# A fifth pair of channels in a feed-forward stage, and weight remainders written by accumulating transfers

## The chip, the cores and the metric

The kernel runs on one core of one Trainium2 chip. A core has TensorE (PE: matmuls and transposes; PEld is its weight load), VectorE (DVE), ScalarE (ACT), GpSimd (POOL) and SyncE (SP), which here only issues transfers. The engines run at the same time, each through its own instructions in order. The metric is the device time of one execution in microseconds, as the median of several runs; lower is better.

## The reference

A decoder trunk of two layers in float32, for 512 tokens of width 1024. The first layer is a Mamba-2 mixer, the second is latent attention; each is followed by a gated feed-forward block, and a layer norm stands behind each of the four.

```python
for i in range(DEPTH):
    if i < N_A_LAYERS:
        mix = ssd_mixer(h, ...)
    else:
        mix = mla_attention(h, q_down[j], q_norm_g[j], q_up[j], attn_out[j], k_nope, k_rope, v, cos, sin)
    h = layer_norm(DN_ALPHA * h + mix, ln_mix_g[i], ln_mix_b[i])
    ff = conv_ffn(h, ffn_up[i], ffn_conv_w[i], ffn_conv_b[i], ffn_down[i])
    h = layer_norm(DN_ALPHA * h + ff, ln_ffn_g[i], ln_ffn_b[i])
    if i == N_A_LAYERS - 1:
        shared_kv = mla_shared_kv(h, kv_down, kv_norm_g, kv_up_k, kv_up_v, cos, sin)

def conv_ffn(h, up, conv_w, conv_b, down):
    u = causal_depthwise_conv(h @ up, conv_w, conv_b)
    g, val = jnp.split(u, 2, axis=-1)
    return (jax.nn.silu(g) * val) @ down
```

The feed-forward block has 2816 hidden channels, 22 groups of 128. The attention has 8 heads, with a query rank of 384, a key/value rank of 256 and a rotary part of 64.

## The kernel before

**Two-part numbers.** TensorE works on a rounded 32-bit format, so each operand is split into a rounded part (`h`, tile `wh` for weights) and a remainder (`l`, tile `wl`). A product is three matmuls: high by high, high by low, low by high (`mm_a` for up projections, `mm_b`, lines 165 to 167, for those with tokens on the rows).

**The weight stream.** `WStream` holds one list of weight items in the order of their use. SyncE loads an item into a staging tile `wst`; `_split` makes `wh` with a ScalarE cast (line 96) and `wl` with a VectorE subtraction (line 97). `wh` and `wl` have six slots each, and an item's slot is free when the product of the item six places earlier is done. `ahead` and `get` say how far ahead of the product the split stands in program order. Items of the kinds "r", "a", "+", "-" are sums and differences of weight blocks, made in a tile `rs` by transfers: the kind "a" is an accumulating transfer that POOL issues (line 52).

**The stages.** The mixer ends at about 412 us. The first feed-forward stage runs to about 770, the attention to about 953, the second feed-forward stage to the end.

**A feed-forward stage** (`ffn`) takes its channel groups in two rounds and then the rest. In a round, the up projection computes channels (two banks of 24 matmuls for each), with convolution, activation and split on ScalarE and VectorE. Neighbouring channels form a pair, and `down_pairs` multiplies the pairs by their down weights with seven products of half-token blocks for two output halves, where the plain way has eight (a Strassen-like scheme: `pair_operands` makes the sums of activations, the weight stream those of weights). The table `RP0` (first stage) or `RP1` (second stage) lists the pairs: ((2, 2, 1), (2, 1, 1)) is five pairs in the first round and four in the second, and numbers in brackets are the pairs that share one weight item. Channels beyond the pairs go through plain pieces (`piece`), one for each token tile of 128 and output half, with the residual add (line 185) and the layer norm behind them: a mean (189), a sum of squares on ScalarE (194), a small POOL part, two steps on VectorE for each half (210 and 215). `transpose_h` turns a normed token tile into `ht` with eight transposes (274), a ScalarE cast (277) and a VectorE subtraction (278). Two tiles are transposed within the stage, two are put off (`k.pend`) into the attention.

**The attention** (`mla`) first projects down (`down`, 16 steps of three matmuls for a token tile, weights `dw`), transposes the compressed rows, and makes V and the rotary queries. Then it goes head by head: `qk` for the next head (weights `hw`, 640 wide, or the staged split of an output weight, 1024 wide, later on), `qk_rope` for every second head, `pv` of the head before (its output is copied to `oT`, ScalarE line 1307, VectorE line 1308), `ptrans` (transposes of the probabilities E to PT, lines 1288 to 1291), `scores` of the next head. Two `ws.ahead` calls in each head place the splits. Last come the output pieces (`out_piece`): the first two items of the output weights `aow` for all token tiles, then, after the last head's `pv`, the other six.

**What sets the order.** Each engine's instructions are put in order by a scheduler at build time; only SyncE's keep the order of the program. `issue_after` ties a split to a point of the other work.

Of the kernel before, what the change touches and what calls it, by code (L numbers as in the profile page):

```python
# [18 lines left out]
P = 128  # L19
# [10 lines left out]

class WStream:


# [42 lines left out]
    def _split(self, nst=None):  # L76
# [19 lines left out]
        nc.scalar.copy(h[:, :f], s[:, :f])  # L96
        nc.vector.tensor_tensor(l[:, :f], s[:, :f], h[:, :f], op=ALU.subtract)  # L97
        self.w[i] = (h, l)
# [188 lines left out]

RP0 = ((2, 2, 1), (2, 1, 1))
RP1 = ((2, 2, 1), (2, 1, 1))


def rounds(rp):
    r0 = 2 * sum(rp[0])
    return r0, r0 + 2 * sum(rp[1])


def ffn_items(up, down, rp):

    it = []
    R0, R1 = rounds(rp)
    dv = down.rearrange("(k p) n -> p k n", p=P)
    for r, ks in enumerate((range(R0), range(R0, HT))):
        for c in ks:
            it.append((up[c], 1024))
            it.append((up[c + HT], 1024))

        for odd, hf, kinds in ((0, 0, "r"), (0, 1, "a"), (1, 1, "+="), (0, 0, "-"), (1, 0, None), (1, 0, "a")):
            j = ks[0]  # L310
            for p, n in enumerate(rp[r]):
                b = dv[:, j:j + 2 * n, hf * 512:(hf + 1) * 512].rearrange("p (k e) n -> p k e n", e=2)[:, :, odd, :]
                it += [(b, n * 512, kind, p) for kind in kinds or (None,)]
                j += 2 * n
    for hf in range(2):
        for j in range(R1, HT, 2):
            it.append((dv[:, j:j + 2, hf * 512:(hf + 1) * 512], 1024))
    return it
# [41 lines left out]

def down_pairs(k, ws, n, prs, parts, first, between):

# [3 lines left out]
    nc = k.nc  # L366
    X, Y, Z = ([k.bank() for _ in range(2)] for _ in range(3))
    ni = len(parts)
# [23 lines left out]
    def ahead(n, ins):  # L392

        with k.tc.issue_after(ins.ins):
            ws.ahead(n)
# [3 lines left out]
    n += ni  # L399
    ahead(n, add(X, 0, 0, 1))  # L400
    for p in range(ni):
        product(Y, "s1", p, n + p, True, True)
    n += ni
    ahead(n, add(Y, 1, 1, 1))
    between()
    for p in range(ni):
        product(X, "s2", p, n + 2 * p, False, True)
        product(Y, "s4", p, n + 2 * p + 1, False, True)
    n += 2 * ni
    add(X, 0, 1, -1)  # L410
    ahead(n, add(Y, 0, 1, 1))
# [8 lines left out]
def ffn(k, ws, base, cwp, gb, rp, la=2, out=None, mid=None):  # L420

    nc, tc = k.nc, k.tc
    R0, R1 = rounds(rp)
    with ExitStack() as c:
        pool = lambda n, b: c.enter_context(tc.tile_pool(name=n, bufs=b))
        pools = {"gt": pool("gt", 18), "fw": pool("fw", 7), "rs": pool("rs", 1), "cw": pool("cw", 1)}
        k.junk = (pools["fw"], "acc")
# [17 lines left out]
        for r in range(2):  # L445
# [5 lines left out]
            def finish(ci, bg, bv):  # L451
# [8 lines left out]
                j = len(prs)  # L460
                a11, a2, s12, s34 = half[j // 2][:, j % 2], new_gt(), new_gt(), new_gt()
                pair_operands(k, pools, even.pop(), av, a11, a2, s12, s34)
# [4 lines left out]
            if k.pend:  # L467
# [19 lines left out]
                c0 += 2  # L487
            for ci in range(c0, HT if r else R0):
                bg, bv = k.bank(), k.bank()
                ws.ahead(n + 1)  # L490
                for b, i in ((bg, n), (bv, n + 1)):
                    w = [x.rearrange("p (k m) -> p k m", k=KT) for x in ws.get(i)]
                    k.mm_a(b, w, k.ht, slice(0, 512))
                    ws.retire(i)
                n += 2
                ws.ahead(n)
                finish(ci, bg, bv)
            if mid and not r:
                mid()
            n = down_pairs(k, ws, n, prs, rp[r], not r, norm_params if r else lambda: None)  # L500
        if out is None:
# [23 lines left out]
        for i in range(NT):  # L525
# [20 lines left out]
            k.add_mix(i, 1, b, 1.0, True)  # L546
            if out is None and i >= 2:
                k.transpose_h(i - 2)
            xn[i] = row("xn")
# [11 lines left out]
    if out is None:  # L561
        k.pend = [lambda: k.transpose_h(NT - 2), lambda: k.transpose_h(NT - 1)]
    return n
# [9 lines left out]
LAG = [20, 18, 7.6, 5, 7.6, 13]  # L573
DRAM = bass.MemoryType.DRAM


# [488 lines left out]
def mla_items(dw, vw, rw, hw, ow):  # L1065

    it = [(dw[j], 1024) for j in range(4)] + [(dw[j][:, :768], 768) for j in (4, 5)]
    rv = rw.rearrange("(k p) n -> p k n", p=P)
    it += [(rv[:, 0:2, :], 1024), (rv[:, 2:3, :], 512)]
    vv = vw.rearrange("(k p) n -> p k n", p=P)  # L1070
    it += [(vv[:, :, hf * 512:(hf + 1) * 512], 1024) for hf in range(2)]
    it += [(hw[h], 640) for h in range(AH)]
    it += [(ow[j * P:(j + 1) * P, :], 1024) for j in range(AH)]
    return it
# [47 lines left out]
def mla(k, ws, base, ngp, gb):  # L1122
    nc, tc = k.nc, k.tc
    with ExitStack() as cx:
# [18 lines left out]

        def down(i):
            bq, bk = k.bank(), k.bank()
# [9 lines left out]
            seen = set()  # L1155
            for c, (j, o, kk, off, w) in enumerate(plan):
                wh, wl = ws.get(n[0] + j)
                last = o.shape[1] == QR and kk == 7 or o.shape[1] != QR and kk == 7
# [59 lines left out]
        for i in range(NT):  # L1218
            down(i)
            if k.pend:  # L1220
                k.pend.pop(0)()
            if i:
                down_t(i - 1)
# [239 lines left out]
```

## Time and profile before

| what | value |
|---|---|
| median of 3 runs | 1312.31 us (1311.85 to 1312.35) |
| profiled execution | 1311.7 us |
| its span in the trace | 1310.0 us |
| granted TensorE clock | 0.998 |
| PE busy | 1299.5 us, 99% of the span |
| DVE busy | 1020.6 us, 78% |
| ACT busy | 636.0 us, 49% |
| POOL busy | 93.1 us, 7% |

A row of the groups, or of the timeline, names a line, an engine, an operation, the tiles written and read, and shapes; a number in brackets at its end is the idle time ahead of it with what ended it. PE's spans are pipelined, so that the pace of matmuls is the distance of their starts. In the chain of waits each row is a start, a length and what the execution's end depended on then.

### The profile page before, as it was taken

The page shows a single profiled execution, that of the slowest core. Times are in us where ns is not written, and L with a number is a line of the kernel's source. Part 1 is how long each engine was busy: PE and PEld are TensorE (multiplying, and loading weights), DVE is VectorE, ACT ScalarE, POOL GpSimd, SP SyncE. Part 2 cuts the span into 40 slices and gives each one's busy share as a digit, 9 for nine tenths or more (in the row PEclk, how much of TensorE's full clock was granted, in tenths as well). Part 3 has the DMA queues.
Part 4 walks back from the last instruction along what each step waited for, and adds up shares of the span by engine and source line. Part 5 has one row for each costly group of instructions (what it writes and reads, how often), then busy time and mean ns, then how long its engine had stood idle before and what let it go on. Part 6 is the DMA issues. An engine that isn't in the chain of part 4 may idle for free.

```text
span 1310.0 us, 17422 instructions
## 1 busy us (share of the span) xinstructions
PE 1299.5 (99%) x6666; PEld 1098.9 (84%) x6666; DVE 1020.6 (78%) x1581; ACT 636.0 (49%) x1029; POOL 93.1 (7%) x96
## 2 busy tenths in 40 slices
PE   9999999999999999999999999999999999999997
PEld 8888888888888988888888899888898888888886
DVE  7888888797798868866766876898587686667587
ACT  6765555455453544444443434665254444444341
POOL 0111011011011001100000012000100010000000
PEclk9999999999999999999999999999999999999999
DMA  8423322313410433352311822121144227323251
GB/s 297 179 113 129 113 88 90 132 58 133 161 65 10 171 129 81 80 207 98 123 58 31 254 81 62 71 107 49 35 149 135 79 35 213 130 97 105 41 161 65
DMA packets 49779, 144.59 MB, mean 110 GB/s; under 512 B 5312, under 2 KB 6336, under 8 KB 48416
## 3 DMA queue, kind: packets, MB, share of 16 engines
q1 hardware_dynamic: 44480, 133.57, 28.8%
q0 software_dynamic: 5072, 9.77, 4.4%
q8 instruction: 52, 0.85, 0.3%
q14 instruction: 31, 0.25, 0.1%
q10 hardware_dynamic: 144, 0.15, 0.0%
HBM read 141.30 MB, written 2.16 MB: 110 GB/s over the span
## 4 chain that ended last, share of the span: by engine, by line
PE 95%; DVE 4%; ACT 1%; issue 0%; DVEq 0%; ACTq 0%
PE ps L159 57%; PE ps L165 10%; PE ps L167 10%; PE ps L166 10%; PE ps L803 1%; PE ps L915 1%; PE ps L811 1%; PE ps L274 1%; PE ps L792 1%; PE ps L742 1%; PE ps L1265 1%; DVE wl L97 1%; DVE PT L1291 1%; PE ps L770 1%; DVE E L1279 0%; DVE smx L1275 0%
## 5 line engine op out<-in xcount | busy, mean ns | idle before, releaser
L159 PE MATMUL ps<-ht,wh 128*128 128x512 f32 (+1 forms) x2256 | 517.0, 379 | 0.0
L159 PEld LDWEIGHTS ps<-ht,wh 128*128 128x128 f32 x2256 | 408.1, 188 | 79.7 <-issue 1.4
L97 DVE TENSOR_TENSOR wl<-wst,wh 128x1024 fp32r<-128x1024 f32 (+3 forms) x222 | 256.3, 1169 | 44.2 <-ACT wh L96 43.3
L96 ACT CAST wh<-wst 128x1024 fp32r<-128x1024 f32 (+3 forms) x222 | 218.8, 995 | 114.3 <-PE ps L167 62.3
L159 PE MATMUL ps<-ht,wl 128*128 128x512 f32 (+1 forms) x1128 | 266.6, 378 | 0.0
L159 PEld LDWEIGHTS ps<-ht,wl 128*128 128x128 f32 x1128 | 205.2, 188 | 39.6
L328 DVE SCALAR_TENSOR_TENSOR acc<-ps,cw,acc 128x511 f32<-128x511 f32 x88 | 65.7, 747 | 80.0 <-ACT acc L327 80.0
L165 PE MATMUL ps<-wh,gt 128*128 128x512 f32 (+1 forms) x320 | 123.7, 387 | 0.0
L167 PE MATMUL ps<-wh,gt 128*128 128x512 f32 (+1 forms) x320 | 123.6, 386 | 0.0
L166 PE MATMUL ps<-wl,gt 128*128 128x512 f32 (+1 forms) x320 | 123.6, 386 | 0.0
L340 ACT CAST gt<-acc 128x512 fp32r<-128x512 f32 (+1 forms) x80 | 44.0, 571 | 102.0 <-DVE acc L333 99.3
L657 DVE SCALAR_TENSOR_TENSOR cv<-ps,cw,cv 128x511 f32<-128x511 f32 (+2 forms) x96 | 71.3, 746 | 26.8 <-ACT cv L655 25.9
L327 ACT ACTIVATE acc<-ps,cw 128x512 f32<-128x512 f32 x88 | 68.3, 776 | 29.5 <-PE ps L159 29.4
L167 PEld LDWEIGHTS ps<-wh,gt 128*128 128x128 f32 x320 | 60.1, 188 | 12.3
L332 ACT ACTIVATE acc<-acc 128x512 f32<-128x512 f32 x44 | 27.8, 632 | 87.6 <-DVE acc L329 87.5
L165 PEld LDWEIGHTS ps<-wh,gt 128*128 128x128 f32 x320 | 60.1, 188 | 12.1
L166 PEld LDWEIGHTS ps<-wl,gt 128*128 128x128 f32 x320 | 60.1, 188 | 12.1
L329 DVE SCALAR_TENSOR_TENSOR acc<-ps,cw,acc 128x510 f32<-128x510 f32 x88 | 65.8, 748 | 2.5
L52 POOL DMA_DIRECT2D rs<-in_down_dram x24 | 25.4, 1058 | 572.7 <-DVE wl L97 572.7
L96 ACT CAST wh<-rs 128x1024 fp32r<-128x1024 f32 (+1 forms) x48 | 39.9, 834 | 46.4 <-DVE rs L88 27.1
L341 DVE TENSOR_TENSOR gt<-acc,gt 128x512 fp32r<-128x512 f32 (+1 forms) x80 | 48.8, 627 | 13.5 <-ACT gt L340 13.5
L387 DVE SCALAR_TENSOR_TENSOR h<-h,ps 128x512 f32<-128x512 f32 x56 | 37.6, 686 | 26.0 <-PE ps L167 26.0
(242 smaller groups left out, 1744.7 us busy)
## 6 DMA issues: line engine op xcount, KB each, us to landing
wst<-in_up_dram SPq DMA_DIRECT2D x88, 512.0 KB, 3.5
wst<-in_xbc_dram SPq DMA_DIRECT2D x32, 512.0 KB, 6.0
wst<-in_down_dram SPq DMA_DIRECT2D x26, 512.0 KB, 5.5
W<-cumd SPq DMA_DIRECT2D x8, 1024.0 KB, 4.6
wst<-in_sow_dram SPq DMA_DIRECT2D x16, 512.0 KB, 3.6
wst<-in_zw_dram SPq DMA_DIRECT2D x14, 512.0 KB, 6.1
rs<-in_down_dram POOLq DMA_DIRECT2D x12, 512.0 KB, 6.9
wst<-in_down_dram SPq DMA_DIRECT2D x18, 256.0 KB, 2.6
```

Source lines behind the costliest of these rows:

```text
L96: nc.scalar.copy(h[:, :f], s[:, :f])
L97: nc.vector.tensor_tensor(l[:, :f], s[:, :f], h[:, :f], op=ALU.subtract)
L159: nc.tensor.matmul(out, w[:, k, :], xts[k][:, x, ts], start=first and p == 0 and k == 0, stop=last and p == 2 and k == nk - 1, skip_group_ ...
L165: nc.tensor.matmul(out, xt[:, 0, tsl], wh, start=start, stop=False, skip_group_check=True)
L166: nc.tensor.matmul(out, xt[:, 0, tsl], wl, start=False, stop=False, skip_group_check=True)
L167: nc.tensor.matmul(out, xt[:, 1, tsl], wh, start=False, stop=stop, skip_group_check=True)
L327: nc.scalar.activation(a, b, AF.Identity, bias=cw[:, ch, 3:4], scale=cw[:, ch, 2:3])
L328: nc.vector.scalar_tensor_tensor(a[:, 1:], b[:, :SEQ - 1], cw[:, ch, 1:2], a[:, 1:], op0=ALU.mult, op1=ALU.add)
L329: nc.vector.scalar_tensor_tensor(a[:, 2:], b[:, :SEQ - 2], cw[:, ch, 0:1], a[:, 2:], op0=ALU.mult, op1=ALU.add)
L340: k.nc.scalar.copy(dst[:, 0, :], src)
L341: k.nc.vector.tensor_tensor(dst[:, 1, :], src, dst[:, 0, :], op=ALU.subtract)
L657: nc.vector.scalar_tensor_tensor(t[:, d:], b[:, :SEQ - d], cw[:, ch, 3 - d:4 - d], t[:, d:], op0=ALU.mult, op1=ALU.add)
```

## The change

`RP0` now has five pairs in both rounds, so that two plain channels are left (20 and 21). The activations' pool holds 18 tiles, too few for everything at once: the two plain channels are computed within `down_pairs`, behind its first product (`late`), two of the banks are taken later, and the load of the norm's parameters (`between`) moves behind two more products. The stage transposes one token tile itself; the other three are put off into the down projection of the attention, one into each of the first three token tiles, at step 11 of 16. A new kind "d" of weight item makes `wl` with a ScalarE copy scaled by -1 and an accumulating POOL transfer from `wst`. It is used for 21 items of the attention: six `dw`, seven `hw` (not the first), eight `aow`.

```diff
@@ WStream._split
         nc.scalar.copy(h[:, :f], s[:, :f])
-        nc.vector.tensor_tensor(l[:, :f], s[:, :f], h[:, :f], op=ALU.subtract)
+        if kind == "d":
+            nc.scalar.activation(l[:, :f], s[:, :f], AF.Copy, scale=-1.0)
+            nc.gpsimd.dma_start(l[:, :f], s[:, :f], accum_op=ALU.add)
+        else:
+            nc.vector.tensor_tensor(l[:, :f], s[:, :f], h[:, :f], op=ALU.subtract)
@@
-RP0 = ((2, 2, 1), (2, 1, 1))
+RP0 = ((2, 2, 1), (2, 2, 1))
 RP1 = ((2, 2, 1), (2, 1, 1))
+NGT = 18
 def rounds(rp):
     r0 = 2 * sum(rp[0])
-    return r0, r0 + 2 * sum(rp[1])
+    r1 = r0 + 2 * sum(rp[1])
+    return r0, r1, min(HT, r1 + NGT - 3 * sum(rp[1]) - (sum(rp[1]) + 1) // 2)
@@ down_pairs
     ahead(n, add(X, 0, 0, 1))
+    n = late(n)
+    Y = new_banks()
     for p in range(ni):
         product(Y, "s1", p, n + p, True, True)
     n += ni
     ahead(n, add(Y, 1, 1, 1))
-    between()
     for p in range(ni):
         product(X, "s2", p, n + 2 * p, False, True)
         product(Y, "s4", p, n + 2 * p + 1, False, True)
     n += 2 * ni
+    between()
+    Z = new_banks()
@@ ffn
-            if out is None and i >= 2:
-                k.transpose_h(i - 2)
+            if out is None and i == 2:
+                k.transpose_h(0)
...
-        k.pend = [lambda: k.transpose_h(NT - 2), lambda: k.transpose_h(NT - 1)]
+        k.pend = [lambda i=i: k.transpose_h(i) for i in range(1, NT)]
@@
+MID = 11
@@ mla_items
-    it = [(dw[j], 1024) for j in range(4)] + [(dw[j][:, :768], 768) for j in (4, 5)]
+    it = [(dw[j], 1024, "d") for j in range(4)] + [(dw[j][:, :768], 768, "d") for j in (4, 5)]
...
-    it += [(hw[h], 640) for h in range(AH)]
-    it += [(ow[j * P:(j + 1) * P, :], 1024) for j in range(AH)]
+    it += [(hw[h], 640) + ("d",) * (h > 0) for h in range(AH)]
+    it += [(ow[j * P:(j + 1) * P, :], 1024, "d") for j in range(AH)]
@@ mla.down
             for c, (j, o, kk, off, w) in enumerate(plan):
+                if mid and c == MID:
+                    mid()
...
-            down(i)
-            if k.pend:
-                k.pend.pop(0)()
+            down(i, k.pend.pop(0) if k.pend else None)
```

How this moves instructions is seen at three places. The first is VectorE at the end of the first feed-forward stage. `L185` is the residual add and `L189` the mean, `L210` and `L215` are the two steps of the norm, `L278` is the low part of a transposed tile; in the changed kernel the same lines are 190, 194, 215, 220 and 283. Before:

```order
L185 SCALAR_TENSOR_TENSOR h,lnst<-h,ps 128x512
L189 TENSOR_SCALAR lnst<-lnst 128x1
L210 SCALAR_TENSOR_TENSOR xn<-h,lnst,lng 128x512
L278 TENSOR_TENSOR ht<-ps,ht 128x4x128 x2
L210 SCALAR_TENSOR_TENSOR xn<-h,lnst,lng 128x512
L97 TENSOR_TENSOR wl<-wst,wh 128x1024
L185 SCALAR_TENSOR_TENSOR h,lnst<-h,ps 128x512
L215 SCALAR_TENSOR_TENSOR h<-xn,lnst,lnb 128x512 x2
L97 TENSOR_TENSOR wl<-wst,wh 128x1024
L97 TENSOR_TENSOR wl<-wst,wh 128x768 x2
```

The changed kernel, from the first plain piece's add on:

```order
L190 SCALAR_TENSOR_TENSOR h,lnst<-h,ps 128x512 x2
L194 TENSOR_SCALAR lnst<-lnst 128x1
L215 SCALAR_TENSOR_TENSOR xn<-h,lnst,lng 128x512 x2
L190 SCALAR_TENSOR_TENSOR h,lnst<-h,ps 128x512
L220 SCALAR_TENSOR_TENSOR h<-xn,lnst,lnb 128x512 x2
L190 SCALAR_TENSOR_TENSOR h,lnst<-h,ps 128x512 x2
L194 TENSOR_SCALAR lnst<-lnst 128x1
L190 SCALAR_TENSOR_TENSOR h,lnst<-h,ps 128x512
L215 SCALAR_TENSOR_TENSOR xn<-h,lnst,lng 128x512 x2
L220 SCALAR_TENSOR_TENSOR h<-xn,lnst,lnb 128x512 x2
L283 TENSOR_TENSOR ht<-ps,ht 128x4x128 x2
```

The remainders `wl` are gone from VectorE here, and tile 0's low parts now stand behind the whole norm of tile 1.

The second place is ScalarE in a head with a rotary tile: `qrT` are the rotary queries, `oT` is the output of the head before, `PT` are the transposed probabilities. Before:

```order
L1251 ACTIVATE qrT_7709<-ps 64x512
L1251 ACTIVATE qrT_7712<-ps 64x512
L96 CAST wh<-wst 128x1024
L1307 CAST oT<-ps 128x512
L1290 CAST PT_7742<-ps 128x512
```

The changed kernel:

```order
L1275 ACTIVATE qrT_7717<-ps 64x512
L1275 ACTIVATE qrT_7720<-ps 64x512
L97 CAST wh<-wst 128x1024
L99 ACTIVATE wl<-wst 128x1024
L1331 CAST oT<-ps 128x512
L1314 CAST PT_7751<-ps 128x512
```

A pass for `wl` now stands between the cast and the copy of `oT`. VectorE's order in the heads is the old one without its rows for `wl`.

The third place is TensorE in the first output piece behind the last head: `wh_8322` and `wl_8323` are the seventh item of the output weights, `wh_8346` and `wl_8347` the eighth, `ps_8353` and `ps_8354` the two output halves. Before (there the two items are 8309, 8310 and 8332, 8333, and the halves 8338 and 8339):

```order
L165 MATMUL ps_8338<-wh_8309,oT_8232 128x512
L166 MATMUL ps_8338<-wl_8310,oT_8232 128x512
L167 MATMUL ps_8338<-wh_8309,oT_8232 128x512
L165 MATMUL ps_8338<-wh_8332,oT_8328 128x512
L166 MATMUL ps_8338<-wl_8333,oT_8328 128x512
L167 MATMUL ps_8338<-wh_8332,oT_8328 128x512
L165 MATMUL ps_8339<-wh_7838,oT_7734 128x512
```

The changed kernel:

```order
L170 MATMUL ps_8353<-wh_8322,oT_8245 128x512
L171 MATMUL ps_8353<-wl_8323,oT_8245 128x512
L172 MATMUL ps_8353<-wh_8322,oT_8245 128x512
L170 MATMUL ps_8353<-wh_8346,oT_8342 128x512
L170 MATMUL ps_8354<-wh_7847,oT_7743 128x512
L171 MATMUL ps_8354<-wl_7848,oT_7743 128x512
L172 MATMUL ps_8354<-wh_7847,oT_7743 128x512
L170 MATMUL ps_8354<-wh_7982,oT_7867 128x512
L171 MATMUL ps_8353<-wl_8347,oT_8342 128x512
```

Four matmuls of the other half have moved ahead of the last item's remainder. On ScalarE the order for these two items is `wl`, `wh`, `wh`, `wl`, where it was two casts.

More of the change, by code (lines that the diff above doesn't have):

```diff
@@ L284, in flush @@
         self.pend = []
-RP0 = ((2, 2, 1), (2, 1, 1))
+RP0 = ((2, 2, 1), (2, 2, 1))
 RP1 = ((2, 2, 1), (2, 1, 1))
+NGT = 18
 def rounds(rp):
     r0 = 2 * sum(rp[0])
-    return r0, r0 + 2 * sum(rp[1])
+    r1 = r0 + 2 * sum(rp[1])
+    return r0, r1, min(HT, r1 + NGT - 3 * sum(rp[1]) - (sum(rp[1]) + 1) // 2)
 def ffn_items(up, down, rp):
     it = []
-    R0, R1 = rounds(rp)
+    R0, R1, RL = rounds(rp)
     dv = down.rearrange("(k p) n -> p k n", p=P)
[L304 to L307, printed above, removed]
+    ups = lambda cs: [(up[c + e], 1024) for c in cs for e in (0, HT)]
+    for r, ks in enumerate((range(R0), range(R0, RL))):
+        it += ups(ks)
         for odd, hf, kinds in ((0, 0, "r"), (0, 1, "a"), (1, 1, "+="), (0, 0, "-"), (1, 0, None), (1, 0, "a")):
@@ L314, in ffn_items @@
                 j += 2 * n
+            if r and kinds == "r":
+                it += ups(range(RL, HT))
     for hf in range(2):
@@ L358, in pair_operands, with down_pairs @@
     split(k, s34, v)
-def down_pairs(k, ws, n, prs, parts, first, between):
+def down_pairs(k, ws, n, prs, parts, first, late, between):
     nc = k.nc
-    X, Y, Z = ([k.bank() for _ in range(2)] for _ in range(3))
+    new_banks = lambda: [k.bank() for _ in range(2)]
+    X = new_banks()
     ni = len(parts)
@@ L422, in ffn @@
     nc, tc = k.nc, k.tc
-    R0, R1 = rounds(rp)
+    R0, R1, RL = rounds(rp)
     with ExitStack() as c:
         pool = lambda n, b: c.enter_context(tc.tile_pool(name=n, bufs=b))
-        pools = {"gt": pool("gt", 18), "fw": pool("fw", 7), "rs": pool("rs", 1), "cw": pool("cw", 1)}
+        pools = {"gt": pool("gt", NGT), "fw": pool("fw", 7), "rs": pool("rs", 1), "cw": pool("cw", 1)}
         k.junk = (pools["fw"], "acc")
@@ L460, in finish @@
                 j = len(prs)
-                a11, a2, s12, s34 = half[j // 2][:, j % 2], new_gt(), new_gt(), new_gt()
+                a11, s12, s34, a2 = half[j // 2][:, j % 2], new_gt(), new_gt(), new_gt()
                 pair_operands(k, pools, even.pop(), av, a11, a2, s12, s34)
@@ L487, in ffn, with channels @@
                 c0 += 2
[L488 to L497, printed above, removed]
+            def channels(cs, n):
+                for ci in cs:
+                    bg, bv = k.bank(), k.bank()
+                    ws.ahead(n + 1)
+                    for b, i in ((bg, n), (bv, n + 1)):
+                        w = [x.rearrange("p (k m) -> p k m", k=KT) for x in ws.get(i)]
+                        k.mm_a(b, w, k.ht, slice(0, 512))
+                        ws.retire(i)
+                    n += 2
+                    ws.ahead(n)
+                    finish(ci, bg, bv)
+                return n
+            n = channels(range(c0, RL if r else R0), n)
             if mid and not r:
                 mid()
-            n = down_pairs(k, ws, n, prs, rp[r], not r, norm_params if r else lambda: None)
+            late = lambda n: channels(range(RL, HT), n) if r else n
+            n = down_pairs(k, ws, n, prs, rp[r], not r, late, norm_params if r else lambda: None)
         if out is None:
@@ L1142, in mla, with down @@
         tok = {}
-        def down(i):
+        def down(i, mid):
             bq, bk = k.bank(), k.bank()
```

## The prediction

> **What bounds the kernel now.** I read the page first: shares of busy time, then the chain of work that ended last.
>
> ```profile
> PE 1299.5 (99%) x6666; PEld 1098.9 (84%) x6666; DVE 1020.6 (78%) x1581; ACT 636.0 (49%) x1029; POOL 93.1 (7%) x96
> ...
> PE 95%; DVE 4%; ACT 1%; issue 0%; DVEq 0%; ACTq 0%
> ```
>
> TensorE sets the time: only a matmul taken away, or a wait of TensorE that appears or goes, moves the end. A saved VectorE microsecond is worth nothing by itself. Next, the busy times by stage: the first feed-forward stage's second up projection, its plain down pieces with the layer norm, the attention heads, and the rest of the attention's output projection.
>
> ```profile
> 579.00:710.00 131.00, 131.00 (x580) 108.47 (x579) 88.15 (x122) 57.04 (x79) 2.96 (x3) 1.00 0.31 97
> 750.00:770.00 20.00, 20.00 (x94) 16.62 (x93) 16.98 (x33) 7.54 (x11) 2.67 (x6) 1.00 0.19 61
> 821.00:907.00 86.00, 84.43 (x487) 73.90 (x485) 80.46 (x206) 56.58 (x139) 1.80 (x1) 1.00 0.24 86
> 908.00:953.00 45.00, 45.00 (x215) 37.64 (x213) 27.39 (x49) 11.45 (x19) 5.08 (x6) 1.00 0.08 27
> ```
>
> The columns are the window, its length, and the busy time of PE, PEld, DVE, ACT and POOL. PE is full in three of them. Only in the heads does it wait, with VectorE busy for 80.46 of 86 us; the waits of TensorE in the heads are these:
>
> ```profile
> PE ps L1288 <- DVE E L1279: 1.0, 2, 0.7
> PE ps L1265 <- DVE oT L1308: 0.8, 3, 0.3
> PE ps L1265 <- DVE kT L1236: 0.2, 1, 0.2
> ```
>
> So no more than 2.0 us can be won there, and everywhere else near the change nothing but matmuls that go.
>
> **The pairs.** Channels 18 and 19 become a fifth pair: seven half-token products for both output halves take 7 x 2 x 3 = 42 matmuls, where the two plain channels took 2 x 8 x 3 = 48. Six matmuls of 512 columns go. Their pace is read from 60 of them in a row:
>
> ```profile
> 750.06 0.39 PE L167 MATMUL ps<-wh,gt 128*128 128x512 f32 x1
> ...
> 763.66 0.39 PE L167 MATMUL ps<-wh,gt 128*128 128x512 f32 x1
> ```
>
> (763.66 - 750.06) / 60 = 0.227 us each: **-1.4 us**. The pair's operands, sums of weights and wider splits give VectorE some 6 us more between 579 and 750 (an estimate from the 1.22 us of a 1024-wide subtraction below: four wide subtractions' worth and some narrow ones). They are hidden while VectorE has 131.00 - 108.47 = 22.5 us free in the up projection alone. The first round has five pairs already and goes from its last channel into the products with a full PE, so I cost the new order of late channels, banks and the moved parameter load at nothing. If that cover failed, PE would wait for the last pair's operands, at most about a microsecond.
>
> **The end of the feed-forward stage.** Each plain piece now has 6 matmuls, 1.36 us, and a token tile 2.72 us rather than 5.44. VectorE's layer norm does not shrink:
>
> ```profile
> 753.94 0.21 DVE L189 TENSOR_SCALAR lnst<-lnst 128x1 f32<-128x1 f32 x1
> 754.19 1.42 DVE L210 SCALAR_TENSOR_TENSOR xn<-h,lnst,lng 128x512 f32<-128x512 f32 x2
> ...
> 755.93 0.69 DVE L185 SCALAR_TENSOR_TENSOR h<-h,ps 128x512 f32<-128x512 f32 x1 [0.32 <-PE ps L167]
> ...
> 756.54 1.41 DVE L215 SCALAR_TENSOR_TENSOR h<-xn,lnst,lnb 128x512 f32<-128x512 f32 x2
> ...
> 763.90 1.03 PE L274 MATMUL ps<-ident,h 128*128 128x128 f32 x8
> ...
> 764.53 1.08 ACT L277 CAST ht<-ps 128x512 fp32r<-128x512 f32 x2 [3.60 <-PE ps L274]
> ...
> 765.75 1.28 DVE L278 TENSOR_TENSOR ht<-ps,ht 128x512 fp32r<-128x512 f32 x2
> ```
>
> Per tile it needs two adds of about 0.75 with the accumulator's read, 0.21, 1.42 and 1.41: 4.5 us. Before, PE's 5.44 us per tile hid that; now VectorE lags. Count from the first plain piece. PE ends six pieces at 8.2, tile 0's transposes at 9.0 and two more pieces at 11.8, then starts the attention's down projection. In the new VectorE order the add of tile 0's second half ends at 3.7 (it waits for PE), mean and first norm half end at 5.3, the next add at 6.0, and tile 0's second norm half, which starts 2.6 us after the mean (756.54 - 753.94), at 7.7. Two adds, the mean, an add and tile 1's first half take it to 11.3; tile 1's second half runs 11.6 to 13.0; only then come the two subtractions for tile 0's low parts, the first of which ends at 13.6. PE can first do four matmuls of the high parts (1408 columns, 0.6 us) and two transposes (0.2), and so wants that part at 12.6. **+1.0 us**, between 0.5 and 1.2 with where the second half starts, and 0 if VectorE catches up somewhere.
>
> **The remainders.** Of 21 weight items, ScalarE now writes the negated, rounded weights and a POOL transfer adds the staged weights onto them: VectorE loses a subtraction, ScalarE gains a pass, and the landing replaces VectorE's end. The prices:
>
> ```profile
> L97 DVE TENSOR_TENSOR wl<-wst,wh 128x1024 fp32r<-128x1024 f32 x11 | 13.4, 1223 | 0.7 <-ACT wh L96 0.7
> L96 ACT CAST wh<-wst 128x1024 fp32r<-128x1024 f32 x12 | 12.5, 1048 | 8.0 <-PE ps L167 7.8
> L96 ACT CAST wh<-wst 128x768 fp32r<-128x768 f32 x2 | 1.7, 840 | 0.8 <-PE ps L167 0.8
> L52 POOL DMA_DIRECT2D rs<-in_down_dram x1: 1213/1213/1213, 513.7 to 513.7; - x1
> DMA to landing us min/median/max: 5.6/5.6/5.6
> L52 POOL DMA_DIRECT2D rs<-in_down_dram x1: 900/900/900, 690.4 to 690.4; - x1
> DMA to landing us min/median/max: 4.0/4.0/4.0
> L52 POOL DMA_DIRECT2D rs<-in_down_dram x1: 1197/1197/1197, 543.8 to 543.8; - x1
> DMA to landing us min/median/max: 8.0/8.0/8.0
> ```
>
> These are accumulating transfers from memory, 512, 256 and 512 KB, the last beside others. One from buffer to buffer is not in this trace. I take 5.6 us for 512 KB (same size, quiet queue), 4.0 as the low end and 8.0 as the high end. For 384 KB, 4.8 lies halfway.
>
> Most items are split far ahead of their use. Two places are not. The down projection's last two items are made by ScalarE after tile 0's casts (11.5), each two passes of 0.84, so their transfers start at 13.2 and 14.9 and land at 18.0 and 19.7. From 13.6 on PE has 11264 columns (22 x 0.227 = 5.0 us) and six transposes (three quarters of eight, 0.6) ahead of the first, 6 x 384 columns (1.0) more ahead of the other: it wants them at 19.2 and 20.2. No loss, with half a microsecond to spare. On POOL's queue both stand ahead of tile 2's variance, but ScalarE's order holds that tile's sum of squares behind the same passes (to 16.2), and its transposes come with the next token tile, ten microseconds later. The other POOL transfers find POOL idle: 1.80 of 86 us in the heads' row, 5.08 of 45 after them.
>
> The other place is the output projection, where there are six remainder slots and the seventh item's comes free only when the first is done:
>
> ```profile
> 915.79 2.00 ACT L96 CAST wh<-wst 128x1024 fp32r<-128x1024 f32 x2 [6.60 <-PE ps L167]
> ...
> 916.27 2.02 PE L1302 MATMUL ps<-PT,ht 128*128 128x512 f32 x12
> ...
> 917.08 2.35 DVE L97 TENSOR_TENSOR wl<-wst,wh 128x1024 fp32r<-128x1024 f32 x2
> ...
> 918.13 0.44 PE L165 MATMUL ps<-wh,oT 128*128 128x512 f32 x1
> ```
>
> Here both last remainders were there at 919.4. On the same clock, the new ScalarE order is remainder, two casts, remainder, one microsecond each from 915.8: the transfers start at 916.9 and 919.8. PE starts the second output piece at 918.13, does 13 matmuls (2.95 us) and wants the first remainder at 921.1; it lands at 916.9 + 5.6 = 922.5, a wait of 1.4. Seven matmuls (1.6 us) later, at 924.1, PE wants the other; it lands at 925.4, a wait of 1.3. Queued behind these are all further output pieces. **+2.7 us**; at a landing of 4.0 it is 0 + 1.1, at 8.0 it is 3.8 + 1.3 = 5.1.
>
> The Trainium skill ("DMA: Bandwidth & Descriptors", section "Anatomy of one DMA — SWDGE (gpsimd) path") fits such a transfer as 2.0 us plus bytes over 436 KB per us, 3.2 us for 512 KB; by that the term would be 0.3 and the whole change a gain of 0.1. The trace disagrees with 5.6 us for the quiet transfer above, and the measurement decides, though it is of a transfer from memory.
>
> **The heads.** VectorE loses 1.22 us in most heads, but where? Two heads, one without and one with the rotary tile:
>
> ```profile
> 855.94 1.05 ACT L96 CAST wh<-wst 128x1024 fp32r<-128x1024 f32 x1
> ...
> 856.87 0.60 ACT L1307 CAST oT<-ps 128x512 fp32r<-128x512 f32 x1
> 857.15 1.22 DVE L97 TENSOR_TENSOR wl<-wst,wh 128x1024 fp32r<-128x1024 f32 x1
> ...
> 858.28 0.68 DVE L1308 TENSOR_TENSOR oT<-ps,oT 128x512 fp32r<-128x512 f32 x1
> ```
>
> ```profile
> 867.40 0.94 ACT wh L96
> ...
> 868.37 1.23 DVE wl L97
> ...
> 869.62 0.70 DVE oT L1308
> ...
> 870.37 0.73 PE ps L1265 x2
> ```
>
> The last four are rows of the chain of waits: PE waited until 870.37 for VectorE's oT, which sat behind the remainder. Now ScalarE puts its new pass between its cast and its oT copy. In the second head: pass 868.3 to 869.3, copy to 869.9, VectorE's oT from 869.9 and not 869.62, 0.28 later. In the first: pass from 857.0 to 857.9, copy to 858.5 against 858.28, 0.2 later. The wait changes its engine and does not go. Yet VectorE has a microsecond more per head for whatever it is behind with, as in the 1.0 us for E. Bounds: all 2.0 us won, or five heads by 0.25, 1.3 us lost. Between them I take **0**.
>
> **The sum.** -1.4 + 1.0 + 2.7 + 0 = +2.3 us on the profiled execution of 1311.7 us (a span of 1310.0 and 1.7 around it): 1314.0. The median of the runs, 1312.31, lies 0.6 above that execution, so 1314.6 us as a median. A measurement of this kernel tells about 0.2%, 2.6 us, from no change: below 1309.7 is faster, above 1314.9 slower.
>
> **Rivals.**
> *Everything hides.* Transfers land in 4 us or less, the layer norm's lag is caught up, and the heads lose all waits: -1.4 - 2.0 = -3.4, 1308.9 us. For it: the profile shows the heads' VectorE nearly full. Against it: the ScalarE pass on the chain, and the 5.6 us.
> *Quick transfers alone.* At 4.0 us the output term is 1.1: -1.4 + 1.0 + 1.1 = +0.7, 1313.0 us. The 256 KB row speaks for it, its size against it.
> *Slow transfers.* A transfer that reads and writes the buffers takes as long as the crowded one, 8.0 us: 5.1 in the output projection, and in the down projection (6.9 for 384 KB by the same ratio) 0.9 + 0.7. -1.4 + 1.0 + 5.1 + 1.6 = +6.3, 1318.6 us. With the other terms as above, the change counts as slower from a landing of 5.9 us on. Against it: the output stage has a DMA share of 0.08 only.
> *ScalarE's pass lengthens every head.* -1.4 + 1.0 + 2.7 + 1.3 = +3.6, 1315.9 us.
>
> **How the numbers follow.** The forecast gets 0.46, rather nearer to no change than to slower (0.28 and 0.18), since its middle is 0.3 us below the border. Everything hides: 0.20, faster. Quick transfers: 0.16, no change. Slow transfers: 0.10, and long heads: 0.08, both slower. So faster 0.20, no change 0.44, slower 0.36. The forecast's own range is 1312.5 to 1316.5 (landing 4.5 to 6.5 us, heads within 1 us). The range that should hold the time 8 times in 10 reaches from the rival where everything hides to most of the slow one: 1308.8 to 1317.5.
>
> **What would show it.** In the new profile: 6 matmuls fewer and 0.227 us each; a wait of PE of about 1 us on VectorE's ht at the start of the down projection; two waits of PE on transfers of wl in the output projection, 1.4 and 1.3 us; landing times of POOL's transfers near 5.6 us; in the heads, waits of PE on oT that stay, those on E that shrink. Wrong would be: landings under 4.2 us, when the first output wait vanishes; no wait for ht; or waits in the heads that sum to under 1 us or over 3.5.

## The result, and the profile after

| | median | range | ratio to before, 95% interval |
|---|---|---|---|
| before | 1312.15 us (10 runs) | 1311.85 to 1312.97 | |
| changed | 1315.66 us (10 runs) | 1314.60 to 1316.34 | 1.0025 (1.0016 to 1.0033) |

The change costs 3.5 us, a quarter of a per cent. The prediction was 1314.6 us, inside the bound for no change, with slower as the second likeliest. The measured median lies in the forecast's own range (1312.5 to 1316.5) and 0.8 us above the border of 1314.9 from which the prediction speaks of slower. The profiled execution of the changed kernel took 1315.76 us with a span of 1314.0; the one before took 1311.7 with 1310.0.

The page first, engines and chain:

```profile
PE 1300.1 (99%) x6660; PEld 1097.4 (84%) x6660; DVE 1003.5 (76%) x1564; ACT 655.1 (50%) x1050; POOL 111.6 (8%) x117
...
PE 96%; DVE 1%; DMA 1%; ACT 1%; issue 0%; SPq 0%; POOL 0%; DVEq 0%; ACTq 0%; POOLq 0%
```

Six matmuls fewer, as the pair promised; VectorE 17 us less busy, ScalarE 19 and POOL 18.5 more. VectorE's share of the chain fell from 4% to 1%, and the end is later all the same. Next, the busy times of the stages around the change (window, length, then PE, PEld, DVE, ACT and POOL, the clock, the share of the DMA engines and their GB/s):

```profile
750.00:772.00 22.00, 21.41 (x101) 17.68 (x99) 15.16 (x29) 14.62 (x19) 5.70 (x9) 1.00 0.79 191
822.00:910.00 88.00, 85.78 (x495) 74.92 (x494) 69.32 (x196) 66.53 (x153) 11.55 (x13) 1.00 0.53 133
910.00:956.00 46.00, 44.47 (x207) 36.52 (x206) 24.30 (x47) 12.98 (x21) 6.81 (x8) 1.00 0.25 66
```

In the first and third, where PE was full before, it now idles. In the heads VectorE has 18.7 us free in 88, and PE does not get more done. TensorE's waits from the first feed-forward stage to the end of the attention:

```profile
PE ps L1289 <- DVE oT L1332: 1.9, 2, 1.0
PE ps L171 <- DMA wl<-wst: 1.4, 1, 1.4
PE ps L172 <- DVE ht L283: 0.8, 1, 0.8
PE ps L1289 <- DVE kT L1260: 0.2, 1, 0.2
```

**Where the 4.0 us of the two spans lie.** I compared the starts of the same work in both traces. The first transposes of normed tokens, which end work that the change does not touch, start at 412.26 before and 413.75 after: 1.5 us. From there to the last transposes of the compressed rows (814.54 and 815.82) the changed kernel wins 0.2. From those to the last head's probability transposes (906.42 and 908.56) it loses 0.9. From those to the first transposes behind the output projection (934.52 and 938.46) it loses 1.8. The rest is alike to 0.1. So the change costs 2.5 us behind that point in these two traces, and 1.5 us belong to the start, to which the last of the experiments returns.

**The end of the feed-forward stage,** in the chain of waits of the changed kernel:

```profile
768.94 0.55 POOL lnst L208
...
769.58 0.56 POOL lnst L209
...
770.16 1.41 DVE h L220 x2
771.58 0.61 DVE ht L283
...
772.23 0.59 PE ps L172 x2
```

PE's distance from one matmul to the next shows a wait of 0.99 us here and 0.11 more behind it: tile 1's second norm half, then tile 0's low part, then PE, in that order.

**A rotary head,** in the chain of waits of the changed kernel:

```profile
868.82 0.52 PE ps L1289 x5
...
869.34 1.06 ACT wl L99
...
870.42 0.59 ACT oT L1331
...
871.04 0.70 DVE oT L1332
...
871.79 1.42 PE ps L1289 x5
```

Where VectorE's `wl` stood between ScalarE's cast and VectorE's oT, ScalarE's `wl` now stands. The wait there grew from 0.42 to 1.11 us.

**The output projection,** in the timeline of the changed kernel:

```profile
917.38 1.06 ACT L99 ACTIVATE wl<-wst 128x1024 fp32r<-128x1024 f32 x1 [6.46 <-PE ps L171]
...
918.74 0.86 POOL L100 DMA_DIRECT2D wl<-wst  x1 [12.93 <-ACT wl L99]
920.23 1.05 ACT L99 ACTIVATE wl<-wst 128x1024 fp32r<-128x1024 f32 x1
...
921.58 0.86 POOL L100 DMA_DIRECT2D wl<-wst  x1 [1.98 <-ACT wl L99]
...
926.53 0.50 PE L171 MATMUL ps<-wl,oT 128*128 128x512 f32 x1 [1.44 <-DMA wl<-wst]
```

PE starts the second output piece at 919.95 here and at 918.13 before, 1.82 us later. On the clock of before, the transfers start at 916.9 and 919.8, as foreseen. They land 4.4 and 4.9 us after their issue:

```profile
L100 POOL DMA_DIRECT2D wl<-wst x1: 862/862/862, 918.7 to 918.7; - x1
DMA to landing us min/median/max: 4.4/4.4/4.4
L100 POOL DMA_DIRECT2D wl<-wst x1: 860/860/860, 921.6 to 921.6; - x1
DMA to landing us min/median/max: 4.9/4.9/4.9
```

PE waits 0.25 us for the first and 1.60 for the second.

### The profile page after: what moved, and what is told of

Same layout as the page of the kernel before. It is cut to its first block, busy times and chain, and to the rows that moved or that the text cites. A ratio compares the mean times of both kernels' runs of the same rounds, so it can differ in the third digit from the quotient of the medians.

```text
span 1314.0 us, 17454 instructions
## 1 busy us (share of the span) xinstructions
PE 1300.1 (99%) x6660; PEld 1097.4 (84%) x6660; DVE 1003.5 (76%) x1564; ACT 655.1 (50%) x1050; POOL 111.6 (8%) x117
## 4 chain that ended last, share of the span: by engine, by line
PE 96%; DVE 1%; DMA 1%; ACT 1%; issue 0%; SPq 0%; POOL 0%; DVEq 0%; ACTq 0%; POOLq 0%
PE ps L164 58%; PE ps L172 10%; PE ps L171 10%; PE ps L170 10%; PE ps L1289 2%; PE ps L827 1%; PE ps L835 1%; PE ps L1326 1%; PE ps L279 1%; PE ps L816 1%; PE ps L766 1%; PE ps L1312 1%; PE ps L939 1%; PE ps L794 1%; DMA xst<-in_xT_dram 0%; DMA wl<-wst 0%
## 5 line engine op out<-in xcount | busy, mean ns | idle before, releaser
L97 ACT CAST wh<-wst 128x1024 fp32r<-128x1024 f32 (+4 forms) x220 | 217.9, 1001 | 104.3 <-PE ps L172 54.8
L102 DVE TENSOR_TENSOR wl<-wst,wh 128x1024 fp32r<-128x1024 f32 (+3 forms) x199 | 232.6, 1182 | 41.8 <-ACT wh L97 39.8
```

## The experiments

The starts of the traces differ, so the table has, beside the median, the span from the first transposes of normed tokens to the end of each profile. Differences are to before. The ratios go by runs of the kernel before made beside each kernel, with medians of 1312.15 to 1312.40 us.

| kernel | median us | ratio, 95% interval | those transposes | span | from there | difference |
|---|---|---|---|---|---|---|
| before | 1312.15 | | 412.26 | 1310.0 | 897.7 | |
| changed | 1315.66 | 1.0025 (1.0016 to 1.0033) | 413.75 | 1314.0 | 900.3 | +2.5 |
| pairs alone | 1315.59 | 1.0028 (1.0017 to 1.0038) | 413.11 | 1313.9 | 900.8 | +3.1 |
| transfers alone | 1321.98 | 1.0074 (1.0062 to 1.0087) | 412.50 | 1320.0 | 907.5 | +9.8 |
| last two by VectorE | 1313.38 | 1.0009 (1.0000 to 1.0017) | 413.94 | 1312.4 | 898.5 | +0.7 |
| down projection only | 1312.49 | 1.0004 (0.9995 to 1.0013) | 412.44 | 1310.1 | 897.7 | 0.0 |
| changed, again | 1315.46 | 1.0022 (1.0013 to 1.0031) | 413.09 | 1313.4 | 900.3 | +2.5 |
| split later | 1310.08 | 0.9981 (0.9973 to 0.9990) | 412.79 | 1307.5 | 894.7 | -3.1 |
| before, split later | 1310.78 | 0.9988 (0.9979 to 0.9997) | 412.76 | 1309.0 | 896.2 | -1.5 |
| later, tile order | 1309.57 | 0.9981 (0.9972 to 0.9990) | 413.18 | 1307.9 | 894.7 | -3.1 |
| heads only | 1309.30 | 0.9977 (0.9968 to 0.9986) | 413.16 | 1308.0 | 894.9 | -2.9 |
| two down by VectorE | 1310.50 | 0.9987 (0.9978 to 0.9995) | 412.51 | 1308.4 | 895.9 | -1.9 |

### The two halves of the change

The pairs alone: all items of the attention lose their kind "d".

```diff
-    it = [(dw[j], 1024, "d") for j in range(4)] + [(dw[j][:, :768], 768, "d") for j in (4, 5)]
+    it = [(dw[j], 1024) for j in range(4)] + [(dw[j][:, :768], 768) for j in (4, 5)]
-    it += [(hw[h], 640) + ("d",) * (h > 0) for h in range(AH)]
-    it += [(ow[j * P:(j + 1) * P, :], 1024, "d") for j in range(AH)]
+    it += [(hw[h], 640) for h in range(AH)]
+    it += [(ow[j * P:(j + 1) * P, :], 1024) for j in range(AH)]
```

> The changed kernel with every remainder made by VectorE again: the fifth pair, the late channels and the moved transposes stay. Theory (the change is three separate terms: the pairs with the layer norm's lag, late transfers in the output projection, a longer ScalarE path in the heads): heads and output projection as before the change, no wait there beyond the old 2.0 us; at the end of the first feed-forward stage VectorE now also makes four to six remainders of 1.2 us among the norm's steps, so the wait for ht grows from 1.0 to 2 to 5 us; 1.4 us of matmuls saved: 1313 to 1315.5 us. Rival (VectorE catches up there, the lag is the transfers' fault): no wait for ht, 1310.8 us. On the start: in the changed kernel's trace the first long run of matmuls begins 1.5 us later than before the change, in work that the change doesn't touch. If that is chance, this trace may begin it anywhere between 18.1 and 19.6 us; if it comes with the changed program, at 19.6.

Measured: 1315.59 us, just above the theory's range. TensorE's waits between 755 and 800 us in this trace:

```profile
PE ps L279 <- DVE h L220: 1.4, 1, 1.4
PE ps L1211 <- PE ps L172: 0.5, 1, 0.5
PE ps L279 <- DVE h L190: 0.3, 1, 0.3
PE ps L1211 <- DVE ctok L1203: 0.3, 1, 0.3
PE ps L171 <- DVE wl L102: 0.2, 1, 0.2
```

VectorE is late by the remainders' time, but PE pays for it elsewhere than I had written: in front of tile 0's transposes (1.6 us from one matmul to the next), and with smaller waits behind. The pair without the transfers of the down projection is a loss of 3.1 us: the two belong together. The theory of separate terms held for heads and output projection, which are as before.

The transfers alone: kind "d" and its 21 items on the kernel before.

```diff
+        if kind == "d":
+            nc.scalar.activation(l[:, :f], s[:, :f], AF.Copy, scale=-1.0)
+            nc.gpsimd.dma_start(l[:, :f], s[:, :f], accum_op=ALU.add)
+        else:
+            nc.vector.tensor_tensor(l[:, :f], s[:, :f], h[:, :f], op=ALU.subtract)
-    it += [(ow[j * P:(j + 1) * P, :], 1024) for j in range(AH)]
+    it += [(ow[j * P:(j + 1) * P, :], 1024, "d") for j in range(AH)]
```

(The `dw` and `hw` items likewise; nothing else of the change.)

> The kernel before with the 21 transfers, without the fifth pair and without the moved transposes. Theory of three terms: the down projection's remainders land in time; the output projection loses 1.8 us to two late remainders; the heads lose 0.9 us, since waits for oT of 1.1 us take the place of shorter ones: 1314.9 us. Rival (the loss comes with the pairs, the transfers are neutral): 1312.2 us.

Measured: 1321.98 us, 7 us beyond the theory. The heads and the output projection lost as in the changed kernel (two waits of 1.1 us for oT; 0.19 and 1.78 us on the last transfers). The rest, 7.0 us up to the last transposes of the compressed rows, is at the down projection; waits between 755 and 800 us:

```profile
PE ps L170 <- DMA wl<-wst: 4.5, 3, 2.3
```

By the distance from one matmul to the next, PE loses 5.3 us at these three waits. The other 1.7 us stand right behind the last of them, where the row of the busy times has a granted clock of 0.52 instead of 1.00:

```profile
784.00:787.50 3.50, 3.50 (x17) 3.40 (x16) 1.01 (x3) 1.75 (x4) 0.91 (x2) 0.52 0.52 196
```

Matmuls of 384 columns follow each other after 0.32 us there and after 0.17 outside. The other eleven traces have such a clock only in their last 4 to 8 us. What lowered it no run shows.

The landing times in this trace come next, then ScalarE's first rows for the late items:

```profile
wl<-wst POOLq DMA_DIRECT2D x12, 512.0 KB, 5.0
wl<-wst POOLq DMA_DIRECT2D x7, 320.0 KB, 3.9
wl<-wst POOLq DMA_DIRECT2D x2, 384.0 KB, 8.3
```

```profile
766.88 1.05 ACT L96 CAST wh<-wst 128x1024 fp32r<-128x1024 f32 x1
767.82 1.06 ACT L98 ACTIVATE wl<-wst 128x1024 fp32r<-128x1024 f32 x1
```

The old plain pieces hold four of the six slots to their end, so only two items of the down projection can be split ahead, and four are split from 766.88 on, when PE is about to need them. With the pair, the plain pieces hold two slots, and four items are ahead. So the order says that a slot freed earlier makes the transfers bearable there, not the matmuls saved; no run frees the slot without the pair. My prediction had looked only at the order in the changed kernel and so had not seen that the two halves depend on each other in both directions.

### The output projection's late remainders

```diff
-    it += [(ow[j * P:(j + 1) * P, :], 1024, "d") for j in range(AH)]
+    it += [(ow[j * P:(j + 1) * P, :], 1024) + ("d",) * (j < 6) for j in range(AH)]
```

> The changed kernel, with only the last two items of the output weights made by VectorE again. Theory: the waits of 0.25 and 1.6 us on their transfers go, nothing else changes: 1.8 us under the changed kernel, 1313.8 us. Rival (something else holds the output projection, the wait moves to VectorE or ScalarE): 1315 us or more.

Measured: 1313.38 us, 2.3 under the changed kernel by the medians and 1.8 by the spans without their start. No wait of PE is left behind the heads. The theory holds, and with it the term.

### The transfers in the heads

Transfers for the down projection alone:

```diff
-    it += [(hw[h], 640) + ("d",) * (h > 0) for h in range(AH)]
-    it += [(ow[j * P:(j + 1) * P, :], 1024, "d") for j in range(AH)]
+    it += [(hw[h], 640) for h in range(AH)]
+    it += [(ow[j * P:(j + 1) * P, :], 1024) for j in range(AH)]
```

> The changed kernel with transfers for the six items of the down projection alone. Theory: heads and output projection as before the change, the wait for ht at the down projection of 1.0 us as in the changed kernel: before - 1.4 + 1.0 = 1311.8 us, or up to 1.5 us more if the late start belongs to the changed program. Rival (the heads' loss does not come from ScalarE's pass): the waits for oT of 1.1 us stay, 1312.7 us or more.

Measured: 1312.49 us, 0.7 above the theory and inside what it allows for a late start. PE's waits between 822 and 930 us are the old ones, 0.9 for E and 0.7 for oT, and the wait for ht of 0.8 us stays. Against the run with only the last two by VectorE, which differs in the seven head items and the first six output weights, all split in the heads, the trace gains 0.8 us. So the transfers, or ScalarE's passes for them, cost that in the heads. Which of these, the next pair of runs asks. The place of the split within a head is moved:

```diff
                 a, d = qk_rope(h + 1) or ends
-                with tc.issue_after(a.ins), tc.issue_after(d.ins):
-                    ws.ahead(n[0], most=1)
+                if not h:
+                    with tc.issue_after(a.ins), tc.issue_after(d.ins):
+                        ws.ahead(n[0], most=1)
```

From the second head on, only the second `ws.ahead`, behind the copies of PT, makes a split. Once on the changed kernel with the last two items by VectorE, once on the kernel before:

> The kernel with the last two output weights by VectorE, and in the heads from the second on the place of the split moved from ahead of oT's copy to behind the copies of PT, where ScalarE idles some 2 us. Theory (in the heads the loss is ScalarE's pass on the path to oT): the two waits of 1.1 us for oT go, and with VectorE's microsecond free the waits for E too; the sum of TensorE's waits in the heads falls from 2 us to under 0.7: 0.9 us of loss and 1.2 us of old waits less than 1313.4, that is 1311.3 us. Rival (the loss comes with the transfers or ScalarE's load as such): 1313.4 us.

> The kernel before, with only the place of the split in the heads moved behind the copies of PT. Theory (VectorE is nearly full in the heads, so that its remainder delays something wherever it stands): the waits for oT go, those for E grow, the sum stays near 2 us: 1312.2 us within 0.7. Rival (the place alone is what counts): the waits fall under 0.7 us, 1310.9 us.

Measured: 1310.08 and 1310.78 us. ScalarE in a rotary head of the first:

```profile
866.89 0.59 ACT L1331 CAST oT<-ps 128x512 fp32r<-128x512 f32 x1
867.37 1.42 ACT L1314 CAST PT<-ps 128x512 fp32r<-128x512 f32 x4
868.64 1.09 ACT L97 CAST wh<-wst 128x1024 fp32r<-128x1024 f32 x1
869.60 1.10 ACT L99 ACTIVATE wl<-wst 128x1024 fp32r<-128x1024 f32 x1
870.59 0.37 ACT L1301 ACTIVATE E<-ps,smx 128x128 f32<-128x128 f32 x1
```

Both passes now fill the gap between the copies of PT and the first exponential, and oT is copied first. The stage from 822 to 910 us, this kernel and then the kernel before with the split moved:

```profile
822.00:910.00 88.00, 87.85 (x510) 77.98 (x509) 72.69 (x202) 66.54 (x154) 11.54 (x13) 1.00 0.51 127
```

```profile
822.00:910.00 88.00, 86.93 (x505) 76.83 (x504) 83.16 (x212) 58.09 (x143) 1.80 (x1) 1.00 0.25 84
```

With as much work on ScalarE and as many transfers as in the changed kernel, PE now waits for 0.2 us in all (for kT) instead of 2. So it was not the transfers and not the load but the place of the split (cast and pass move together) on the path to oT. In the kernel before, the rival came nearer than my theory, though the waits in its list sum to 1.1 us and not to under 0.7: the place alone is worth 1.5 us by the spans without their start. One wait of 0.9 us for E is left there, at the last head, with VectorE at 83 of 88 us; the transfers, placed well, take that too. What I had not seen is that the place alone, with VectorE's load unchanged, brings about half of what place and transfers win together (2.9 us in the kernel with heads only, below).

### The wait for ht

In the kernel with the later split, tile 1's second norm half is put behind tile 0's transposes:

```diff
-            if i:
+            if i and (out is not None or i != 2):
                 with tc.issue_after(added.ins):
                     ln_b(i - 1, 0)
...
             if out is None and i == 2:
                 k.transpose_h(0)
+                with tc.issue_after(k.ht_lo.ins):
+                    ln_b(1, 0)
+                    ln_b(1, 1)
```

(`ht_lo` is the last low-part subtraction.)

> The kernel with the last two output weights by VectorE and the later split, and at the end of the first feed-forward stage tile 1's second norm half put behind tile 0's transposes, so that VectorE makes tile 0's low parts first. Theory: the wait of 1.0 us for ht shrinks to 0.3 or less: 1310.6 us. Rival (VectorE is behind by the whole tile, not by the order): the wait moves to tile 1's transposes, 1311.3 us.

Measured: 1309.57 us. The wait for ht is gone, and the span without its start is the same as without this edit, 894.7 us: PE now comes a microsecond earlier to the down projection's last two transfers, and by the distance of its matmuls waits 0.14 and 0.70 us for them. In this trace these two land 5.6 and 5.9 us after their issue. Neither theory nor rival: the wait went to the next thing that was late, one that I had costed with half a microsecond to spare.

So these two items were given back to VectorE:

```diff
-    it = [(dw[j], 1024, "d") for j in range(4)] + [(dw[j][:, :768], 768, "d") for j in (4, 5)]
+    it = [(dw[j], 1024, "d") for j in range(4)] + [(dw[j][:, :768], 768) for j in (4, 5)]
```

> The kernel with the later split and the changed tile order, with the last two items of the down projection by VectorE as well. Theory: the waits of 0.14 and 0.70 us on those two transfers go, and since VectorE's 1.9 us for them come before the next tile's norm, part of it comes back as a wait for tile 1's transposes or its low parts: 1309.0 us, within 0.6. Rival (VectorE behind by as much again): 1310.5 us.

Measured: 1310.50 us, the rival's number. The transfers' waits go, and PE waits for the compressed rows instead:

```profile
PE ps L1214 <- DVE ctok L1206: 1.3, 1, 1.3
PE ps L1214 <- PE ps L172: 0.3, 1, 0.3
```

In front of those rows VectorE itself stands idle for the load of `ang`, a transfer that POOL issues only when the last tile's norm is done:

```profile
786.22 0.62 DVE L1201 SCALAR_TENSOR_TENSOR ctok<-ps,css,ang 128x384 f32<-128x384 f32 x1 [4.19 <-DMA ang<-in_ang_dram]
```

Counted from the first transposes of normed tokens, that norm's last step starts 2.5 us later than in the run without this edit, and so do the compressed rows. VectorE's two remainders, 1.8 us, stand ahead of that norm. So the path here goes from VectorE's norm over a load of some 3.5 us to the compressed rows; VectorE's busy time is not the bound (6.3 of 10 us from 775 to 785).

### What the pair is worth

The kernel before with the transfers of the heads and of the first six output weights, and the later split; no pair, no moved transposes, the down projection by VectorE. Beside the new branch of `_split` and the moved split, both shown above:

```diff
-    it += [(hw[h], 640) for h in range(AH)]
-    it += [(ow[j * P:(j + 1) * P, :], 1024) for j in range(AH)]
+    it += [(hw[h], 640) + ("d",) * (h > 0) for h in range(AH)]
+    it += [(ow[j * P:(j + 1) * P, :], 1024) + ("d",) * (j < 6) for j in range(AH)]
```

> The kernel before, without the pair and without the moved transposes; transfers for the seven head items and the first six output weights alone, and the split in the heads behind the copies of PT. Theory: in the heads a transfer is worth its place plus VectorE's microsecond: TensorE's waits there near 0.4 us, as in the run with the later split and the pair; what that run had besides was 1.4 us of matmuls less and 1.0 us of wait for ht. So this one is 0.4 us over it when both starts are alike: 1310.5 us. Rival (the pair carries the gain): 1312 us.

Measured: 1309.30 us, the fastest median of the series, 0.9977 (0.9968 to 0.9986) of before. By the span without the start it is 0.2 us behind the kernel with the pair and the later split. The fifth pair with all that it needs is worth 0.2 us there, where I had said 0.4; by the medians it is worth nothing, since this kernel lies 3.1 us under before and that one 2.3. The intervals of this kernel and of the one with the tile order (0.9972 to 0.9990) overlap, and both lie below before and the changed kernel.

### The start

The changed kernel without any edit:

> The changed kernel itself, once more, for a second profile. So far its trace begins the first long run of matmuls at 19.4 us, the kernel before at 17.9, and four variants at 18.8, 18.2, 19.6 and 18.1. If the start is chance, this trace begins it at another place between 17.9 and 19.7 and the rest of the span is as in the first profile, 1294.6 us from there, with waits of about 1 us for ht, twice 1.1 us for oT, and 0.2 and 1.6 us on transfers. If it belongs to the program, it begins at 19.4 again.

Measured: the same kernel starts its first transposes of normed tokens 0.66 us earlier in the second profile, and the rest agrees to 0.1 us (900.3 and 900.3), with the same waits. Over all twelve traces they start between 412.26 and 413.94 us. It is at least in part chance of an execution. In the chain of the changed kernel's first trace the start hangs on the loads of the input:

```profile
3.11 6.11 DMA xst<-in_xT_dram
```

This load landed 1.5 us earlier before, and so did the one ahead of it and the two behind it, by 1.2 to 1.7 us. The difference of the medians, 3.5 us, is 1.0 above the difference of the spans without their start, and the runs without a profile do not show where they lost it. That programs with the pair start late more often is likely but not shown. In their eight measurements the difference of the medians lies 0.0 to 1.0 us above that of the spans, 0.4 in the mean, and in the three of programs without it 0.0 to 0.2 below; the traces with the pair start those transposes at 413.10 us in the mean, the four without it at 412.67.

## Why the prediction was right or wrong

**The pairs** (-1.4): right. Six matmuls fewer, and no wait at the round's products or late channels. One reading on the way was wrong: the 108.47 us taken for VectorE's busy time are those of the weight load. VectorE's are 88.15, so that it had 42.9 us free and not 22.5, and the operands were hidden all the more easily.

**The end of the feed-forward stage** (+1.0): right in size, place and order, 0.99 + 0.11 us. One detail was off and cancelled: mean to second norm half took 770.16 - 767.31 = 2.85 us and not 2.6, since POOL's first small step took 0.55 us, but the mean came some 0.4 us earlier than counted.

**The down projection's last transfers** (0, with half a microsecond to spare): right in the changed kernel, where the wait for ht came first. 384 KB took 4.9 and 5.4 us, beside others, and not 4.8. The spare hung on that wait: in the run with the other tile order, where it went and the two landed after 5.6 and 5.9 us, they cost the microsecond again.

**The output projection** (+2.7): the mechanism and the starts were right, the size was too large by 0.85, since 512 KB landed after 4.4 and 4.9 us and not 5.6. The term with 4.4 and 4.9 on the prediction's own clock is 0.2 + 1.8 = 2.0; measured, 0.25 + 1.60. It is the quick bound (4.0) that was nearer. The Trainium skill's fit ("DMA: Bandwidth & Descriptors", section "Anatomy of one DMA — SWDGE (gpsimd) path") gives an estimate of 3.2 us for this size; the measurements, 4.4 and 4.9, lie between it and the row that I used.

**The heads** (0): this is the step that failed. The prediction set a lengthened path to oT against a freer VectorE and took the middle. Measured: +0.9, by the distance of PE's matmuls against the run with the later split, where these waits are gone. In two rotary heads the wait for oT grew by 0.69 and 0.61 us (1.11 against 0.42 and 1.12 against 0.50). From the start of ScalarE's cast to the start of VectorE's oT it is 2.64 us there, where it was 2.32: 0.32 more, close to the 0.28 that I had worked out. The rest of the growth comes mostly from PE, which reaches this wait sooner after the cast than before. Elsewhere the gains and losses are smaller, each with the later matmul behind the wait: the wait for E of 0.87 us went, as hoped, and one of 0.42 for oT in a later head, but a new wait of 0.33 for oT and two of 0.27 for E came. So the freer VectorE gave less than the longer path took. The rival of the longer ScalarE path had the mechanism and the nearer size (+1.3), though not the spread of it over five heads.

**The sum.** -1.4 + 1.1 + 1.85 + 0.9 = +2.45 against +2.3: two errors of 0.9, one in the output projection and one in the heads, cancelled. That the sum came out so well is luck. The remaining 1.0 of the measured 3.5 us is in none of these terms; the start is the likely place, and the prediction did not have it.

**The rivals.** Everything hides: no, but the split behind PT shows that its 2.0 us in the heads were there to be won. The later split even won 2.4 us between the last transposes of the compressed rows and those of the last head, so the prediction's bound was too low: the list of waits does not count that the matmul behind a wait comes some 0.1 us late. Quick transfers alone: half right in the landing, wrong in the heads. Slow transfers: in the changed kernel no; in the run with the transfers alone, 384 KB took 8.3 us, and the loss was larger than this rival's.

## What to carry to other kernels

Taking work from a nearly full engine pays only if what replaces it is not put on the same chain of waits: ask of the new pass what stands behind it on its own engine, and put it where that engine idles. A transfer that replaces an engine's last step needs its landing time of lead, some 5 us here, so items whose buffer comes free late are to be left with the engine. When two edits share a ring of buffers, cost each alone as well: here the transfers without the pair cost 7 us more than with it.

## What was not expected of the hardware

An accumulating transfer from buffer to buffer of 512 KB had a median of 5.2 us from issue to landing in the changed kernel, where those from memory had 5.9:

```profile
rs<-in_down_dram POOLq DMA_DIRECT2D x14, 512.0 KB, 5.9
wl<-wst POOLq DMA_DIRECT2D x12, 512.0 KB, 5.2
...
wl<-wst POOLq DMA_DIRECT2D x7, 320.0 KB, 3.9
...
wl<-wst POOLq DMA_DIRECT2D x2, 384.0 KB, 5.2
```

In the timeline of the kernel before, the first small step of the layer norm on POOL has this row:

```profile
755.59 0.18 POOL L203 TENSOR_SCALAR lnst<-lnst 128x1 f32<-128x1 f32 x1 [29.50 <-ACT lnjunk L194]
```

The same step, of 128 numbers, took 0.55 us at 768.94 in the changed kernel, while VectorE ran a norm step with two inputs from the buffer (768.04 to 769.45), and again 0.55 us at 774.32 beside the next such step (773.42 to 774.83). At 755.59 that VectorE step was all but over (754.19 to 755.61). The Trainium skill ("SBUF — State Buffer", section "Who interferes with whom") says that a VectorE instruction with two such inputs contends with a GpSimd instruction that reads the buffer; the two rows agree, though no run here took the one away to see the other shrink.
